# Products of the unscaled activations at six norms, with the order of ScalarE and VectorE there written out

## The chip, the cores and the metric

The kernel runs on one core of a Trainium2 chip. The metric is the device time of one execution in microseconds; the kernel before took 1698.53 us (median of three runs, 1694.67 to 1702.13). All matrix products are made in float32 accuracy from float32r operands: each operand is split in a high part `h` (rounded) and a low part `l` (the remainder), and a product is `h·h + l·h + h·l`, so three passes of TensorE (PE) for each pair of tiles.

## The reference, cut to what matters

Two blocks follow each other: the first has two layers (gated DeltaNet, then mLSTM, each with a convolved feed-forward network), the second has a SwiGLU network, a mixing stage of three branches and a second SwiGLU network. Between them stand RMS norms:

```python
def rms_norm(x, w):                                   # the same in both blocks
    y = x * rsqrt(mean(x * x, -1) + 1e-6)             # one factor for each token
    return y * w                                      # one factor for each channel
...
for i in range(2):                                    # first block, 272 tokens, 1024 channels
    mix = gated_deltanet(rms_norm(hs, norm_w[i, 0])) if i == 0 else mlstm(rms_norm(hs, norm_w[i, 0]))
    hs = hs + rms_norm(mix, norm_w[i, 1])
    f = conv_ffn(rms_norm(hs, norm_w[i, 2]))          # (silu(conv(h @ w_gate)) * conv(h @ w_up)) @ w_down
    hs = hs + rms_norm(f, norm_w[i, 3])
...
x = x + 0.5 * swiglu(rmsnorm(x, ffn1_norm), ffn1_w_gu, ffn1_w_down)   # second block, 256 tokens
z = rmsnorm(x, mix_norm) @ w_in                       # 5280 columns: gating, latents, queries, gates
x = x + merged(z) @ w_out
x = x + 0.5 * swiglu(rmsnorm(x, ffn2_norm), ffn2_w_gu, ffn2_w_down)
```

At four places an output norm, the addition to the residual and the next input norm follow each other (after DeltaNet, after the first feed-forward network, after mLSTM, after the second one); at two places (before the mixing stage and before the last SwiGLU) only an addition and an input norm stand there. These are the six norms of the title, numbered 1 to 6 below in order of time.

## The kernel before, in words

Activations lie transposed: eight tiles of 128 channels by 272 (258, 256) tokens, all in `hst`. A weight of 512 KB is loaded by SyncE into one of three `wraw` buffers; ScalarE (ACT) copies its high part to `wh`, VectorE (DVE) or GpSimd (POOL) subtracts to get the low part `wl`; `wh` and `wl` have three buffers each, so a fourth weight waits until PE has done with the first. `wload` (L355) chooses the engine of `wl`: POOL for the first loads after a norm (`POOL_FIRST`) and for every second or fourth load of some stages (`POOL_EVERY`), else DVE.

`linears_g` (L420) makes the first chunk behind a norm: four output tiles at once, 96 products over the eight tiles of its input `X`. Behind it `conv_ffn` (L1395) and `swiglu_up` (L1720) go chunk by chunk: 48 products for the gate, 48 for the up half. Output tiles lie in PSUM, in three buffers of the pool `pp` that go round, and in banks `pc0` to `pc2`, `pb0`, `pb1`. A chunk's tile is read by ACT and DVE (convolution, silu, product with the gate, split into `hh`); until then its bank is not free.

The order of PE is fixed when the kernel is built: `Threads` runs generators against a model of the engines' times and lets whichever has its operands ready go next. The other engines' order is the scheduler's, except inside `manual_schedule`, where it is the order of the code. Each engine works its own queue strictly in that order.

`mix_end` (L694) is a norm of the first four. While the last projection runs, `mix_tile` (L664) adds up squares of the output (`macc`), of the output times its norm weight (`mwacc`) and cross products with the residual (`mcross`). Ones-products on PE add them over channels (tiles `rsp`). `rstd` (L589, a logarithm and an exponential on ACT, and a Newton step on DVE where wanted) makes the factor `r` of the output norm. POOL then updates the residual (`mw` times `r`, added to `hst`), tile by tile; at the same time DVE works out the square sum of the new residual from the three sums (`sqn`, `ssq`) and the factor `r2` of the input norm with a Newton step; then DVE multiplies each tile by weight and `r2` (`xn`), ACT rounds it (high part of `xhl`) and DVE subtracts (low part). `prenorm` (L637) does the same for norms 5 and 6 without an output norm. `warm` products fill a part of the wait at norms 1 and 2; products of the memory branch (`memp`, L1808) fill a part at norms 3, 4 and 5.

`embed` (L748) starts the kernel: 32 `warm` products, the factor of the first input norm from the loaded tokens, products `xp` that transpose and scale them, and the norm weights brought into columns (`columns`, tile `vps`, copied into `pvt`).

Of the kernel before, what the change touches and what calls it, by code (L numbers as in the profile page):

```python
# [208 lines left out]
class Kern:  # L209
    def __init__(self, ctx, tc, ins, out):  # L210
# [23 lines left out]
        self.near_load = self.seg = 0  # L234
        self.gctx = ExitStack()
# [64 lines left out]
    def stt(self, out, a, s, b, op0, op1):  # L300
        self.V.scalar_tensor_tensor(out, a, s, b, op0, op1)
# [117 lines left out]

    def linears_g(self, jobs, K, X, N):  # L420

        ps = [self.ps((128, N)) for _ in range(3)] + [self.bank("pc2", (128, N), "ps")]
        for k0 in range(0, K, 4):
            hl = [self.wload(w, k0, 4, c0, 256) for w, c0, fn in jobs]
            both = list(enumerate(ps))
            for part in [both] if k0 + 4 < K else [both[:2], both[2:]]:
                for k in range(4):
                    xh, xl = X[k0 + k]
                    yield [xl]
                    for j in range(3):  # L430
                        for n, p in part:
                            w = hl[n // 2][j == 1]
                            c = slice(n % 2 * 128, n % 2 * 128 + 128)
                            self.mm(p[:], w[:, k, c], xl if j == 2 else xh, k0 + k == j == 0, k0 + k == K - 1 and j == 2)
        for n, p in enumerate(ps):
            jobs[n // 2][2](n % 2, p[:])
# [200 lines left out]
    def prenorm(self, src, wcol, N, acc):  # L637

        r = self.sm(N, "rstd", "rstd")
        yield self.part_done  # L640
        self.rstd(r[:], (yield from self.colsum_end(0, acc[1]))[:], D, NW[2])
        self.seg += 1
        self.near_load = self.nload + POOL_FIRST[self.seg]
        return self.normed(src, wcol, r, N)
# [19 lines left out]
    def mix_tile(self, m, ps, wcol, N):  # L664
# [15 lines left out]
        if m == KD - 2:  # L680
            self.th.add([self.early([self.macc, self.mwacc, self.mcross], N)])

    def prefetch(self, loads, late=None):
        for w, *a in loads:
            self.ready[w.tensor.name, a[0], a[2]] = self.wload(w, *a[:4], late=late, own=a[4] if a[4:] else None)
# [8 lines left out]
    def mix_end(self, src, wcol, N, loads=(), late=1):  # L694
# [11 lines left out]
        r = self.sm(N, "rstd", "rstd")  # L706
        r2 = self.sm(N, "rstd2", "rstd2")
        u = self.sm(N, "sqn", "y")
        X = self.xslots(N)

        def update(k, op, n=2, eng=None):
            s2 = self.hst[:, k:k + n, T - N:]
            w = self.mw[k // 2][:, k % 2:k % 2 + n, :N]
            if op == ALU.mult:
                self.tt(w, w, r[:, None, :].to_broadcast([128, n, N]), op, eng)
            else:
                self.tt(s2, s2, w, op, eng)

        low = []
# [1633 lines left out]
```

## Time and profile before

| | |
|---|---|
| median of 3 runs | 1698.53 us (1694.67 to 1702.13) |
| the profiled execution | 1692.27 us |
| its span, first to last instruction | 1690.5 us |
| PE busy | 1563.8 us (93%) |
| DVE busy | 1093.2 us (65%) |
| ACT busy | 925.3 us (55%) |
| POOL busy | 625.4 us (37%) |
| mean granted TensorE clock | 0.968 of full speed |

The share of busy time says which engine has most to do in all; it doesn't say which engine sets the pace in a given stretch. That is read from stretches around a norm: how long it takes from the last product in front of it to the 96th behind it, and what PE waits for in between.

### The profile page before, as it was taken

To read this page: it belongs to the slowest core of one execution; us is meant where nothing else is said; L and a number is where in the kernel's file an instruction comes from. 1 tells how busy PE (TensorE), PEld (TensorE's weight loads), DVE (VectorE), ACT (ScalarE), POOL (GpSimd) and SP (SyncE) were. 2 spreads that over 40 slices of the span, in tenths; PEclk is the share of its full clock that TensorE was granted. 3 is DMA by queue.
4 is the path that set the end of the run, shared out by engine and by line. 5 is a ranking of instruction groups with operands and counts; after the bars stand their busy time and mean duration, and the time that the engine had idled before them with its cause. 6 is when DMAs were issued, how large, how long until landed. Compare 5 with 4: busy or idle time off the path is not lost.

```text
span 1690.5 us, 31083 instructions
## 1 busy us (share of the span) xinstructions
PE 1563.8 (93%) x11945; PEld 1473.4 (87%) x11945; DVE 1093.2 (65%) x2121; ACT 925.3 (55%) x1877; POOL 625.4 (37%) x575
## 2 busy tenths in 40 slices
PE   8889888889899998899899998999997899999999
PEld 6778777789799997788799997999986799989987
DVE  3788977757788756357777667545459653465543
ACT  3467767656466544446566555544444664554442
POOL 2675554330500003551544444212265648512221
PEclk7889999999999999999999999999999999999999
DMA  4322221226365553444356654656554435546564
GB/s 131 101 76 63 76 64 51 76 76 198 94 182 169 170 174 93 108 120 138 109 179 188 186 176 126 199 174 194 181 161 138 115 99 151 179 147 186 181 193 150
DMA packets 239098, 235.38 MB, mean 139 GB/s; under 512 B 11510, under 2 KB 226406, under 8 KB 238950
## 3 DMA queue, kind: packets, MB, share of 16 engines
q1 hardware_dynamic: 238326, 231.86, 45.5%
q8 instruction: 94, 1.54, 0.4%
q0 software_dynamic: 496, 1.41, 0.3%
q14 instruction: 54, 0.44, 0.1%
q10 hardware_dynamic: 128, 0.13, 0.0%
HBM read 232.32 MB, written 1.05 MB: 138 GB/s over the span
## 4 chain that ended last, share of the span: by engine, by line
PE 69%; DVE 20%; ACT 5%; issue 2%; DMA 2%; POOL 1%; ACTq 0%; DVEq 0%; POOLq 0%
PE ps L190 54%; PE pst L190 5%; DVE cy L190 3%; DVE rq_a L190 3%; ACT wh L190 2%; DVE RT L190 1%; DVE wl L190 1%; DVE rq_y L190 1%; DVE xhl L190 1%; POOL wl L381 1%; DVE xn L190 1%; PE xp L190 1%; DVE nwa L190 1%; DMA wraw<-in_ffn_w_up_dram 1%; DVE on L190 1%
## 5 line engine op out<-in xcount | busy, mean ns | idle before, releaser
L190 PE MATMUL ps<-xhl,wh 128*128 128x256 f32 (+2 forms) x4624 | 882.8, 293 | 33.7 <-ACT xhl L190 17.3
L190 PEld LDWEIGHTS ps<-xhl,wh 128*128 128x128 f32 x4624 | 721.6, 192 | 43.7 <-ACT xhl L190 19.4
L190 ACT CAST wh<-wraw 128x1024 fp32r<-128x1024 f32 (+2 forms) x436 | 447.8, 1029 | 388.1 <-PE ps L190 261.4
L190 PE MATMUL ps<-xhl,wl 128*128 128x256 f32 (+2 forms) x2312 | 644.0, 287 | 1.3 <-DVE wl L190 0.8
L381 POOL TENSOR_TENSOR wl<-wraw,wh 128x512 fp32r<-128x512 f32 (+3 forms) x264 | 335.2, 1294 | 524.5 <-ACT wh L190 501.7
L190 PEld LDWEIGHTS ps<-xhl,wl 128*128 128x128 f32 x2312 | 435.6, 192 | 1.9 <-DVE wl L190 1.0
L190 DVE TENSOR_TENSOR wl<-wraw,wh 128x1024 fp32r<-128x1024 f32 (+2 forms) x237 | 289.2, 1221 | 208.4 <-ACT wh L190 202.1
L190 POOL TENSOR_TENSOR wl<-wraw,wh 128x512 fp32r<-128x512 f32 x134 | 173.9, 1320 | 145.5 <-ACT wh L190 132.8
L190 PE MATMUL ps<-hh,wh 128*128 128x256 f32 (+1 forms) x1056 | 191.1, 283 | 0.0
L190 PEld LDWEIGHTS ps<-hh,wh 128*128 128x128 f32 x1056 | 163.2, 189 | 0.0
L190 PE MATMUL ps<-hh,wl 128*128 128x256 f32 (+1 forms) x528 | 149.7, 284 | 0.0
L190 DVE SCALAR_TENSOR_TENSOR fy<-ps,pvt,fy 128x256 f32<-128x256 f32 (+2 forms) x176 | 85.0, 488 | 25.0 <-ACT fy L190 23.1
L190 PEld LDWEIGHTS ps<-hh,wl 128*128 128x128 f32 x528 | 99.5, 188 | 0.0
L190 DVE SCALAR_TENSOR_TENSOR cy<-cx,pvt,cy 128x271 f32<-128x271 f32 (+2 forms) x96 | 74.6, 780 | 14.2 <-ACT cy L190 13.2
L190 DVE TENSOR_TENSOR hh<-fy,hh 128x256 fp32r<-128x256 f32 (+1 forms) x88 | 65.2, 744 | 14.0 <-ACT hh L190 13.9
L190 POOL MEMSET mvt<- 128x4 f32 x4 | 0.4, 103 | 177.2 <-PE ps L190 177.2
L298 POOL TENSOR_TENSOR mw<-mw,rstd 128x544 f32<-128x544 f32 (+5 forms) x20 | 24.1, 1205 | 111.1 <-ACT rstd L190 111.1
L190 ACT ACTIVATE fy<-ps,pvt 128x272 f32<-128x272 f32 (+1 forms) x88 | 49.6, 569 | 12.1 <-PE ps L190 11.7
L190 PE MATMUL pst<-wh,hh 128*128 128x512 f32 x176 | 55.0, 393 | 0.0
L190 ACT CAST hh<-fy 128x256 fp32r<-128x256 f32 (+1 forms) x88 | 35.6, 406 | 29.4 <-DVE fy L190 28.8
L190 DVE CAST_PREDICATED RT<-lvl,w 128x512 f16<-128x512 uint8 x67 | 44.9, 683 | 7.1 <-PE w L190 6.9
L190 PE MATMUL ps<-og,wh 128*128 128x272 f32 x256 | 48.6, 289 | 0.1
(510 smaller groups left out, 2353.7 us busy)
## 6 DMA issues: line engine op xcount, KB each, us to landing
wraw<-in_ffn_w_up_dram SPq DMA_DIRECT2D x88, 512.0 KB
wraw<-in_ffn_w_gu_dram SPq DMA_DIRECT2D x88, 512.0 KB
wraw<-in_ffn_w_down_dram SPq DMA_DIRECT2D x79, 512.0 KB
wraw<-in_gdn_w_in_dram SPq DMA_DIRECT2D x48, 512.0 KB
wraw<-in_w_in_dram SPq DMA_DIRECT2D x41, 512.0 KB
wraw<-in_ml_w_in_dram SPq DMA_DIRECT2D x24, 512.0 KB
wraw<-in_gdn_w_out_dram SPq DMA_DIRECT2D x16, 512.0 KB
wraw<-in_ml_w_out_dram SPq DMA_DIRECT2D x8, 512.0 KB
```

What stands on the lines that cost most here:

```text
L190: r = f(*args, **kw)
L298: (eng or self.V).tensor_tensor(out, a, b, op)
L381: eng.tensor_tensor(l[:, a, b], r[:, a, b], h[:, a, b].bitcast(F32), ALU.subtract)
```

## The change

Since the factor of an input norm is the same for all channels of a token, it can be applied to the product's result. At norms 1 to 4 the residual is now updated by DVE, and ACT and DVE make the operand from the residual and the norm weight alone (`xr`, high and low part), without the factor `r2`. The factor is worked out later, on DVE behind the eight tiles (`token_scale`, called by `linears_g` through `self.mid`), and DVE multiplies each result by it when it leaves PSUM (`py`). In the two convolved networks and in mLSTM the first chunks (three, and q, k and v of the first two column blocks) use the unscaled operand, and the scaled operand `xhl` is made beside them (`scaled_operand`). In the SwiGLU networks and in the mixing stage all products use the unscaled operand, and norms 5 and 6 make it tile by tile in `add_tile`. The memory product (6, 7) moves from norm 5 into chunk 9 of the SwiGLU network in front of it. At the start there are 35 `warm` products instead of 32, and `columns` comes behind the factor of the first norm.

```diff
     def linears_g(self, jobs, K, X, N, ready=None):
         for k0 in range(0, K, 4):
-            hl = [self.wload(w, k0, 4, c0, 256) for w, c0, fn in jobs]
+            if k0 and self.mid:
+                with self.tc.issue_after(self.last_low.ins), self.tc.manual_schedule(
+                        engines={mybir.EngineType.DVE, mybir.EngineType.Activation}):
+                    hl = [self.wload(w, k0, 4, c0, 256, eng=self.V) for w, c0, fn in jobs]
+                    self.mid()
+                self.mid = None
+            else:
+                hl = [self.wload(w, k0, 4, c0, 256) for w, c0, fn in jobs]
...
     def mix_end(self, src, wcol, N, loads=(), late=1, full=True):
...
-        pb = yield from self.colsum_end(1, self.mwacc[1])
-        pa = yield from self.colsum_end(2, self.mcross[1])
+        pb = yield from self.colsum(self.mwacc, N, "pc1")
+        yield ["pc0"]
+        pa = yield from self.colsum(self.mcross, N, "pc0")
         if N == T:
-            yield from self.warm(2, self.macc[0])
+            yield from self.warm(5, self.macc[0])
...
+        def residual(n):
+            self.tt(w[n], w[n], r[:, None, :].to_broadcast([128, w[n].shape[1], N]), ALU.mult)
+            self.tt(s2[n], s2[n], w[n], ALU.add)
+        def high(*ks):
+            for k in ks:
+                self.act(raw[k][0], src[k], AF.Copy, scale=self.pv(wcol + k))
+        def low(*ks):
+            for k in ks:
+                self.last_low = self.stt(raw[k][1], src[k], self.pv(wcol + k), raw[k][0].bitcast(F32), ALU.mult, ALU.subtract)
-        with self.tc.manual_schedule(engines={mybir.EngineType.DVE, mybir.EngineType.Pool}):
+        with self.tc.manual_schedule(engines={mybir.EngineType.DVE, mybir.EngineType.Activation}):
             self.rstd(r[:], pm[:], D, NW[0])
-            for k, n in ((0, 1), (1, 1), (2, 2), (4, 2), (6, 2)):
-                for op in (ALU.mult, ALU.add):
-                    update(k, op, n, self.nc.gpsimd)
...
+            residual(0)
+            high(0)
+            residual(1)
+            high(1)
+            low(0)
+            residual(2)
+            high(2, 3)
+            low(1)
+            wlow = []
+            self.prefetch(loads[late:], wlow, self.V)
+            residual(3)
+            high(4, 5)
+            low(2, 3)
+            for f in wlow:
+                f()
+            residual(4)
+            high(6, 7)
+            low(4, 5, 6, 7)
+        def token_scale():
             self.tt(u[:], pb[:], r[:], ALU.mult)
...
-            if N == T:
-                yield from self.warm(7, c)
             self.rstd(r2[:], c, D, NW[1])
-            for k in range(0, KD, 2):
...
+        self.mid = token_scale
+        return raw, self.scaled_operand(src, wcol, N) if full else None
+    def scaled(self, p, N=S):
+        y = self.sm(N, "py")
+        self.tt(y[:], p, self.r[:], ALU.mult)
+        return y[:]
...
     def embed(self):
-            for _ in range(32):
+            for _ in range(35):
                 self.mm(p[:], self.zero[:, :128], self.zero[:])
...
-            self.columns(self.norms, 0)
             self.tt(ss[:, 0, :], ss[:, 0, :], ss[:, 1, :], ALU.add)
...
+            self.columns(self.norms, 0)
...
     def conv_ffn(self, X, l, N, lead):
-                y = conv(p, 2 * c + m)
+                y = conv(self.scaled(p, N) if c < 3 else p, 2 * c + m)
...
+                    ps = [self.bank(b, (128, N), "ps") for b in ("pc0", "pc1")] if c == 1 and fn is gate else None
+                    yield from self.linear_g(W, c0, 256, KD, x, N, fn, ps)
+                    if len(X) < KD:
+                        X = next(todo) and next(todo)
...
     def ml_gates(self, X, done):
+        yield [self.r[:], "pb1"]
+        p = self.bank("pb1", (128, 3, 128), "mrp")
+        for t, (o, P) in enumerate(TT):
+            self.tr(p[:P, t, :], self.r[:, o:o + P])
...
     def add_tile(self, m, ps, scale):
-        self.stt(x, ps, scale, x, ALU.mult, ALU.add)
+        if scale == 0.5:
+            y = self.sm(S, "ady", "y")
+            self.stt(y[:], ps, scale, self.r[:], ALU.mult, ALU.mult)
+            self.tt(x, x, y[:], ALU.add)
+        else:
+            self.stt(x, ps, scale, x, ALU.mult, ALU.add)
+        h, l = self.nextX[m]
+        self.act(h, x, AF.Copy, scale=w)
+        self.stt(l, x, w, h.bitcast(F32), ALU.mult, ALU.subtract)
...
     def mem_kv(self):
-        for n, js in enumerate(((0, 1), (2, 3), (6, 7))):
+        for n, js in enumerate(((0, 1), (2, 3))):
```

The order on VectorE at norm 1, before: from the last cross product (`cross`) straight to the square sum of the new residual (`sqn`, `ssq`), the Newton step (`nwv`, `nwa`, `rstd`) and the first scaled tiles (`xn`).

```order
L190 TENSOR_TENSOR cross<-hst,mw 128x272
L190 TENSOR_TENSOR sqn<-rsp,rstd 128x272
L190 SCALAR_TENSOR_TENSOR sqn<-rsp,sqn 128x272
L190 TENSOR_TENSOR sqn<-sqn,rstd 128x272
L190 TENSOR_TENSOR ssq<-sqn,ssq 128x272
L190 TENSOR_SCALAR nwv<-ssq 128x272
L190 TENSOR_TENSOR nwa<-rstd_5992 128x272
L190 TENSOR_TENSOR nwa<-nwa,nwv 128x272
L190 SCALAR_TENSOR_TENSOR rstd_5992<-nwa,rstd_5992 128x272
L190 SCALAR_TENSOR_TENSOR xn<-hst,pvt,rstd_5992 128x272 x2
L190 TENSOR_TENSOR xhl<-xn,xhl 128x272 x2
```

The same place after: the residual (`mw`, `hst`), which POOL had, and the low parts of the unscaled operand (`xr`).

```order
L190 TENSOR_TENSOR cross<-hst,mw 128x272
L190 TENSOR_TENSOR mw<-mw,rstd 128x272
L190 TENSOR_TENSOR hst<-hst,mw 128x272
L190 TENSOR_TENSOR mw<-mw,rstd 128x272
L190 TENSOR_TENSOR hst<-hst,mw 128x272
L190 SCALAR_TENSOR_TENSOR xr<-hst,pvt,xr 128x272
L190 TENSOR_TENSOR mw<-mw,rstd 128x544
L190 TENSOR_TENSOR hst<-hst,mw 128x544
L190 SCALAR_TENSOR_TENSOR xr<-hst,pvt,xr 128x272
```

Further on in the same stretch after: the last low parts, the low part of the last weight of the first chunk, the factor, and the first results that leave PSUM.

```order
L190 SCALAR_TENSOR_TENSOR xr<-hst,pvt,xr 128x272 x4
L190 TENSOR_TENSOR wl<-wraw,wh 128x1024
L190 TENSOR_TENSOR sqn<-rsp,rstd 128x272
L190 SCALAR_TENSOR_TENSOR sqn<-rsp,sqn 128x272
L190 TENSOR_TENSOR sqn<-sqn,rstd 128x272
L190 TENSOR_TENSOR ssq<-sqn,ssq 128x272
L190 TENSOR_SCALAR nwv<-ssq 128x272
L190 TENSOR_TENSOR nwa<-rstd_6006 128x272
L190 TENSOR_TENSOR nwa<-nwa,nwv 128x272
L190 SCALAR_TENSOR_TENSOR rstd_6006<-nwa,rstd_6006 128x272
L190 TENSOR_TENSOR py<-ps,rstd_6006 128x272 x2
```

The factor `r2` (`rstd_6006`, `rstd_5992` before) has moved from in front of the operand to behind it; nothing of a result can be read before it.

The order on ScalarE at norm 4, after (`xr` high parts; `memkt` copies of the memory branch's keys, `junk` their squares; four weights, then the factor `rstd_13078`):

```order
L190 ACTIVATE rstd<-rstd 128x256
L190 ACTIVATE xr<-hst,pvt 128x256 x4
L190 CAST wh<-wraw 128x1024
L190 COPY memkt<-memp 128x512
L190 ACTIVATE xr<-hst,pvt 128x256 x2
L190 COPY memkt<-memp 128x512
L190 ACTIVATE junk,memks<-memkt 128x128 x7
L190 ACTIVATE xr<-hst,pvt 128x256 x2
L190 ACTIVATE junk,memks<-memkt 128x128
L190 CAST wh<-wraw 128x1024 x4
L190 ACTIVATE rstd_13078<-ssq,epst 128x256
```

Seven squares of the memory branch stand in front of the last two high parts, and four weights in front of the factor's logarithm; before, that logarithm stood behind one weight.

The order on PE at norm 2 (mLSTM), before: the transposes of the gate row (`mgp`) stand among the products of the first chunk and wait for no factor.

```order
L190 MATMUL ps<-xhl,wh 128x272 x4
L190 MATMUL ps<-xhl,wl 128x272 x4
L190 MATMUL ps<-xhl,wh 128x272 x4
L190 MATMUL mgp<-eye,gr 128x8 x2
L190 MATMUL mgp<-eye,gr 16x8
L190 MATMUL ps<-xhl,wh 128x272 x4
```

The same place after: transposes of the factor (`mrp`) in front of the last products of the first chunk and of `mgp`.

```order
L190 MATMUL ps<-xr,wl 128x272 x2
L190 MATMUL ps<-xr,wh 128x272 x2
L190 MATMUL mrp<-eye,rstd_8621 128x128 x2
L190 MATMUL mrp<-eye,rstd_8621 16x128
L190 MATMUL ps<-xr,wh 128x272 x2
L190 MATMUL ps<-xr,wl 128x272 x2
L190 MATMUL ps<-xr,wh 128x272 x4
L190 MATMUL ps<-xr,wl 128x272 x2
L190 MATMUL ps<-xr,wh 128x272 x2
L190 MATMUL mgp<-eye,gr 128x8 x2
L190 MATMUL mgp<-eye,gr 16x8
```

PE's queue now waits for `r2` here, with 12 products of the first chunk behind it.

## Rows read from the trace of the kernel before

**Rows 1.** The page: busy time by engine; chain of waits, shares by engine.
```profile
PE 1563.8 (93%) x11945; PEld 1473.4 (87%) x11945; DVE 1093.2 (65%) x2121; ACT 925.3 (55%) x1877; POOL 625.4 (37%) x575
...
PE 69%; DVE 20%; ACT 5%; issue 2%; DMA 2%; POOL 1%; ACTq 0%; DVEq 0%; POOLq 0%
```
**Rows 2.** Stretches: window, length, busy of PE, PEld, DVE, ACT, POOL; clock, DMA, GB/s.
```profile
428.90:458.60 29.70, 22.44 (x126) 19.83 (x126) 21.72 (x30) 11.93 (x22) 18.14 (x15) 0.89 0.18 54
648.00:688.50 40.50, 27.34 (x169) 23.12 (x168) 29.47 (x58) 13.37 (x27) 19.29 (x16) 0.85 0.23 66
808.50:838.10 29.60, 22.36 (x133) 19.62 (x132) 22.24 (x37) 11.78 (x23) 16.74 (x15) 0.88 0.22 70
1021.30:1049.70 28.40, 22.16 (x132) 19.75 (x132) 22.04 (x41) 15.36 (x40) 14.85 (x13) 0.88 0.30 94
1234.40:1255.60 21.20, 20.54 (x144) 18.12 (x143) 11.85 (x26) 10.83 (x22) 13.43 (x15) 1.00 0.48 140
1492.00:1512.00 20.00, 16.75 (x118) 15.70 (x119) 11.75 (x25) 12.10 (x23) 1.97 (x2) 0.91 0.29 87
478.00:490.00 12.00, 12.00 (x98) 12.00 (x97) 10.05 (x17) 7.63 (x12) 0.00 (x0) 1.00 0.60 175
440.90:447.80 6.90, 5.61 (x23) 5.29 (x24) 6.83 (x10) 1.67 (x4) 3.04 (x3) 0.51 0.01 2
```
**Rows 3.** In order of time at norm 1: start, length, engine, operation [idle before <-releaser].
```profile
428.58 0.29 PE L190 MATMUL ps<-og,wl 128*128 128x272 f32 x1
...
429.72 0.43 ACT L190 ACTIVATE sq<-mw 128x272 f32<-128x272 f32 x1
...
431.26 0.43 ACT L190 ACTIVATE rstd<-rstd 128x272 f32<-128x272 f32 x1
...
431.72 0.44 DVE L190 TENSOR_TENSOR sqn<-rsp,rstd 128x272 f32<-128x272 f32 x1 [1.56 <-ACT rstd L190]
...
436.89 1.46 DVE L190 TENSOR_TENSOR nwa<-nwa,nwv 128x272 f32<-128x272 f32 x1
438.01 1.52 POOL L298 TENSOR_TENSOR mw<-mw,rstd 128x544 f32<-128x544 f32 x1
...
441.82 1.27 PE L190 MATMUL ps<-xhl,wh 128*128 128x272 f32 x4 [3.65 <-ACT xhl L190]
...
450.96 2.00 ACT L190 CAST wh<-wraw 128x1024 fp32r<-128x1024 f32 x2 [2.13 <-PE ps L190]
```
**Rows 4.** Groups by shape on DVE: count, busy, mean ns (first three from 478:490).
```profile
L190 DVE TENSOR_TENSOR wl<-wraw,wh 128x1024 fp32r<-128x1024 f32 x4 | 4.9, 1225 | 1.8 <-ACT wh L190 1.6
L190 DVE SCALAR_TENSOR_TENSOR fy<-ps,pvt,fy 128x270 f32<-128x270 f32 x4 | 2.0, 497 | 0.1
...
L190 DVE TENSOR_TENSOR hh<-fy,hh 128x272 fp32r<-128x272 f32 x3 | 1.3, 435 | 0.0
...
L190 DVE TENSOR_TENSOR meml<-wraw,memh 128x512 fp32r<-128x512 f32 x16 | 10.9, 686 | 4.2 <-ACT memh L190 3.9
```
**Rows 5.** In order of time behind norm 1, POOL, DVE and PE.
```profile
461.81 2.75 POOL L381 TENSOR_TENSOR wl<-wraw,wh 128x512 fp32r<-128x512 f32 x2 [1.47 <-ACT wh L190]
...
462.06 2.79 DVE L190 TENSOR_TENSOR fy<-fy,sg 128x272 f32<-128x272 f32 x2
...
467.78 0.49 PE L190 MATMUL ps<-xhl,wh 128*128 128x272 f32 x2 [1.46 <-DVE fy L190]
```
**Rows 6.** Who waited for whom: engine, for what, us, times, longest.
```profile
PE mbp L190 <- DVE mlf L190: 5.3, 1, 5.3
```
**Rows 7.** In order of time at norm 4, ACT.
```profile
1030.16 0.31 ACT L190 ACTIVATE junk<-memkt 128x128 f32<-128x128 f32 x1
1030.37 0.19 ACT L190 ACTIVATION_READ_ACCUMULATOR junk<-memkt 128x1 f32 x1
```
**Rows 8.** Start, in order of time (ACT, PE, DVE), and one stretch as in rows 2.
```profile
8.19 0.19 ACT L190 ACTIVATION_READ_ACCUMULATOR junk<-xt 128x1 f32 x1
...
11.72 0.23 DVE L190 COPY pvt<-vps 128x64 f32<-128x64 f32 x1 [3.79 <-PE vps L190]
...
14.65 13.57 PE L190 MATMUL xp<-rd,xt 128*128 128x128 f32 x48 [2.97 <-DVE rd L190]
...
14.30:34.80 20.50, 19.67 (x75) 16.07 (x76) 7.36 (x15) 3.90 (x8) 2.20 (x4) 0.50 0.42 119
```

More of the change, by code (lines that the diff above doesn't have):

```diff
@@ L312, in act @@
             self.order(inst)
+        return inst
     def split(self, h, l, src):
@@ L635, in normed, with token_scale @@
         return X
-    def prenorm(self, src, wcol, N, acc):
-        r = self.sm(N, "rstd", "rstd")
+    def token_scale(self, acc, N, done):
         yield self.part_done
[L641 to L644, printed above, removed]
+        p = yield from self.colsum_end(0, acc[1])
+        r = self.r = self.sm(N, "rstd", "rstd")
+        self.rstd(r[:], p[:], D, NW[2])
+        yield [r[:], "pc0"]
+        p = self.bank("pc0", (128, 2, 128), "rtp")
+        for t in range(2):
+            self.tr(p[:, t, :], r[:, t * 128:t * 128 + 128])
+        rt = self.rt = self.cst([128, 2], name="rtok", tag="al")
+        self.V.tensor_copy(rt[:], p[:, :, 0])
+        done.set()
     def sumsq(self, go, then):
@@ L680, in mix_tile, with prefetch @@
         if m == KD - 2:
[L681 to L683 removed]
+            self.th.add([self.early([self.macc], N)])
+    def prefetch(self, loads, late=None, eng=None):
         for w, *a in loads:
[L685 removed]
+            self.ready[w.tensor.name, a[0], a[2]] = self.wload(w, *a[:4], late=late, own=a[4] if a[4:] else None, eng=eng)
     def warm(self, n, x):
@@ L1625, in mlstm @@
         self.lane = None
-        yield from self.linears_g([job("q", 0), job("k", 0)], KD, X, T)
+        yield from self.linears_g([job("q", 0), job("k", 0)], KD, raw, T)
+        X = next(todo) and next(todo)
         for kind, n in (("v", 0), ("v", 1), ("q", 1), ("k", 1), ("v", 2), ("v", 3), ("o", 0), ("o", 1), ("o", 2), ("o", 3)):
@@ L1631, in mlstm @@
             else:
-                yield from self.linear_g(w, c0, 256, KD, X, T, fn)
+                yield from self.linear_g(w, c0, 256, KD, raw if (kind, n) in raws else X, T, fn)
+                while len(X) < KD:
+                    next(todo)
+                    if len(X) in (5, 8):
+                        break
         return Y
@@ L1718, in all, with swiglu_up @@
                 return e.value
-    def swiglu_up(self, X, w, extra=None):
+    def swiglu_up(self, X, w, extra=None, late=False, ready=None):
         Y = []
@@ L1737, in swiglu_up @@
             if c == 0:
-                yield from self.linears_g([(w, 0, gate), (w, FF, up)], KD, X, S)
+                yield from self.linears_g([(w, 0, gate), (w, FF, up)], KD, X, S, ready)
             else:
-                yield from self.linear_g(w, c * 256, 256, KD, X, S, gate)
+                ps = [self.bank(b, (128, S), "ps") for b in ("pc0", "pc1")] if c == 1 else None
+                yield from self.linear_g(w, c * 256, 256, KD, X, S, gate, ps)
                 yield from self.linear_g(w, FF + c * 256, 256, KD, X, S, up)
```

127 lines of the change are left out of this document (73 added, 54 removed).

## The prediction

> **What bounds the kernel now.** I read the page first, then one table of stretches, then the order of time around a norm. On the page PE is busy 93% of the span and holds 69% of the chain of waits, DVE 20% [rows 1]: away from the norms PE sets the pace. The steady chunk shows it: 98 products in 12.00 us without a hole, 0.1224 us each, so 96 cost 11.75 us [rows 2]. There DVE is busy 10.05 of 12 us, which matters below.
>
> The table of stretches then runs, for each of the six norms, from the last product in front of it to the 96th behind it. Norm 1 takes 29.70 us for 11.75 us of products, norms 3 and 4 29.60 and 28.40, norm 6 20.00. Norm 2 takes 40.50 us; its stretch holds 24 gate products and a wait for the gates besides. Norm 5 takes 21.20 us, but PE is busy for 20.54 of them: products of the memory branch fill it [rows 2].
>
> The order of time at norm 1 tells why. The last product ends at 428.87 us, the factor's exponential at 431.69, and the first product behind the norm begins only at 441.82: 10.1 us in which DVE works out the second factor beside POOL's residual. There a DVE step that takes 0.44 us alone takes 1.46 [rows 3]. PE then starts at half its clock: 0.51 in the 6.9 us from 440.9 [rows 2], the 1.2 GHz level.
>
> **The change, part by part.**
>
> *First chunk at norms 1 to 4.* ACT's last square ends at 430.15 [rows 3]; logarithm and exponential (some 1.0 us) end at 431.2. Then DVE has, in the order shown: four residual steps of 272 columns, 0.5 us each with the hand-over (2.0); six of 544, from 686 ns for 512 [rows 4] 0.75 each (4.5); eight low parts, 0.45 each from 435 to 497 ns (3.6); one weight remainder, 1.22. Sum 11.3 us, so the last low part ends at 442.5. Two weights of 1.0 us each (2.00 for two [rows 3]) stand before the last two high parts on ACT and wait for PE to leave the first half; I add 1.0: 443.5. The remainder of the last weight, 1.22, ends at 444.7, and 22 to 24 products still come: 447.5. POOL meanwhile takes the next weights; if each of DVE's last steps meets it, 3 us more, 450.5. The 96th product then stands 18.6 to 21.6 us behind the last one in front, against 29.70: 8 to 11 us gained there. The two to five extra warm products and the longer sums fill idle PE: nothing.
>
> *What gives part of it back.* Each result must now wait for `r2`. Behind 444.7 stand eight steps on DVE and two on ACT, 4.5 us alone, up to 10 beside POOL: `r2` at 449 to 455. In chunks 0 to 2 DVE gets twelve multiplications and eight scaled tiles besides. From `r2` to the step that frees the bank of chunk 3's second tile stand 59 DVE instructions: 6 remainders at 1.225 and 53 others at 0.40 (in the steady chunk 13 take 10.05 − 4.9 us [rows 2, 4]), 28.6 us, so 477.8 to 483.6. Before, chunk 3 began at 458.6 + 2 × 11.75 + the 1.46 us of [rows 5] = 483.6, its second tile 1.5 later. So norm 1 keeps 1.5 to 7.3 us; I take 5, the nearer to DVE without POOL, since four loads alone go to POOL. Norm 3 has the same order: 5, range 1 to 8.
>
> A row shows what POOL does to such steps: two of 272 columns took 2.79 us beside a POOL remainder of 2.75 [rows 5], where one alone takes 0.435 [rows 4]. The Trainium skill ("SBUF — State Buffer", section "SBUF: two separate sides") says that a VectorE instruction with two SBUF inputs and a GpSimd instruction exclude each other for their whole length; the trace agrees (1.46 against 1.52 us in turn, rows 3). It speaks against part of this change: the residual leaves POOL, but POOL's four weights now fall on the steps that make `r2`. By it alone `r2` comes at 455 and norm 1 keeps 1.5 us.
>
> *Norm 2.* PE's queue waits for `r2` with 12 products of the chunk behind it, then gates behind that. `r2` at 449 to 455 in norm 1's times, with the same steps; the gate chain from there took PE's 5.3 us wait [rows 6] and lasts as long as before. So the wait for the gates ends about when it did, but 138 products of the projections stand before it where 84 stood: 54 × 0.1224 = 6.6 us are out of the way. I take 5 (0 to 8): what follows is partly a chain of its own.
>
> *Norm 4.* The first chunk as at norm 1, but seven squares of 0.5 us (0.31 + 0.19 [rows 7]) stand before ACT's last high parts: 3.5 us, gain there 7 instead of 9. Then the logarithm of `r2` waits behind four weights, the last of which needs a buffer that PE leaves after the first chunk, and four remainders of the memory branch (0.69 each [rows 4]) stand among the Newton steps. PE has 48 products (5.9 us) in banks of its own, then waits; I put 4 us on it. Gain 3 (−2 to 8). Behind it DVE is light: its multiplications hide under PE.
>
> *Norms 5 and 6.* Seven of eight tiles are ready before the last product, the eighth needs four short steps, some 2.2 us, covered by 84 products. Norm 5 had 0.7 us idle, and its memory products now stand elsewhere at the same cost: 1 (−1 to 2). Norm 6: 20.00 us for 11.75 × 256/272 = 11.1 us of products, 2.5 of transposes and 0.9 of sums: 5.5, and with a clock of 0.91 there [rows 2] I take 6 (4 to 7). The multiplications in SwiGLU and the mixing stage, 68 of about 0.42 us, lie on a DVE with 65% load: nothing, up to 3 if a chain passes through them.
>
> *Start.* The factor's data are ready at 8.38, but DVE stood behind `pvt`, which waited 3.79 us for PE's warm products [rows 8]. The factor comes 3.3 us earlier; warm products (three more, 0.7 us) end at 12.2, and `xp` begins at 12.4 instead of 14.65: 2.2 us. PE had 0.50 of its clock for the 20.50 us from 14.30, though busy for 19.67 [rows 8]; the level fell after the hole of 2.97 us that now closes. If it stays up for the first quarter of `xp`, 1.7 us more: 4 in all; if throughout, half of 13.57 and of the rest, 11. The skill ("TensorE: Matmul & The Clock Gate", Part 1) lets the clock follow how busy PE is; by that it would stay up, while the row shows 96% busy at half the clock. I side with the row.
>
> **Sum.** 4 + 5 + 5 + 5 + 3 + 1 + 6 = 29 us. The profiled execution took 1692.27 us (its span 1690.5), so 1663 in its terms; the runs' median, 1698.53, lies 0.37% above it, and in its terms 1669.5. I say 1669. The bounds of single terms add up to +4 and +51; they will not all fall to one side.
>
> **The rivals.**
>
> *DVE becomes the bound (slower).* Place: chunks 0 to 2 behind norms 1 and 3, the wait for `r2` at norms 2 and 4. DVE there already has 84% load; with 14 us more in three chunks it has over 100%. Price: if the list of 28.6 us runs 1.5 times as long (POOL, waits for ACT), chunk 3 starts some 12 us later than forecast, and a PE hole like the 3.65 us one sets the clock to half for 6.9 us, 3.4 us more. Three such places cost 46 against 29 saved: 1698.5 + 17 = 1715. It decides once the list passes 37 us. For it: the 1.46 us waits behind DVE in [rows 5]. Against it: POOL has four loads, not all.
>
> *The gain stays half.* Norms 1 and 3 keep 1.5 by the exclusion of POOL and DVE, norm 2 keeps 2, norm 4 nothing, the start 2.2, norm 6 5.5: 13 us, 1685.
>
> *Everything fits.* DVE's list hides under PE, no hole lowers the clock: norms 1 to 4 keep 8 each, the start 7, norms 5 and 6 8: 47 us, 1651. Against it: DVE's 46 us of steps from norm 1 to chunk 3 in a stretch of 50.
>
> *It doesn't do what it says.* A first product that still waits for `r2` would give nothing, 1698. The order shows `xr` ahead of the factor, so this is unlikely.
>
> **How the numbers follow.** Forecast (1658 to 1680): 0.48. Half (1680 to 1690): 0.20. Everything fits: 0.14. Nothing left or nothing done (1690 to 1707): 0.11. Slower: 0.07. About 0.5% (8.5 us) is what a measurement can tell here; below 1690 is 0.82, within 0.11, above 1707 0.07. The range leaves out less than 2 in 10: from the middle of the fourth case to the third's, 1650 to 1692.
>
> **What would show it.** Right: the first product behind norm 1 follows the last one in front by about 5 us instead of 13, and the 96th by 19 to 22. `r2` ends 20 to 26 us behind the last product. PE waits for DVE (`py`) in chunks 1 to 3, some us per norm; for `rstd` at norm 2. At norm 6 no hole in front of the first product. `xp` begins near 12.4. Wrong: holes over 10 us in front of chunks 1 to 3, a clock below 0.9 there, or a first product that still waits for `xhl`.

## The result, and the profile after

The changed kernel took 1682.47 us (median of 5 runs, 1679.54 to 1685.82), the kernel before 1696.51 us in runs beside it (median of 5, 1694.67 to 1702.13). The ratio is 0.991, 95% interval 0.989 to 0.994: about 14 us faster, where 29 were forecast. The time lies inside the range given (1650 to 1692), but in the interval of the rival "the gain stays half" (1680 to 1690, given 0.20) and not in that of the forecast (1658 to 1680, given 0.48); the place of the gain is not where either of them had it.

The page after, busy time by engine, answers to [rows 1]:

```profile
PE 1557.9 (93%) x11939; PEld 1470.2 (87%) x11939; DVE 1141.3 (68%) x2284; ACT 936.2 (56%) x1893; POOL 576.6 (34%) x531
```

Stretches after (window, length, busy of PE, PEld, DVE, ACT, POOL; clock, DMA, GB/s), to be held against [rows 2, 8]: the start; norm 1 from the last product in front to the 96th behind it, and from there to the start of chunk 3; the same two at norm 3; norm 4.

```profile
14.30:34.80 20.50, 19.00 (x128) 16.71 (x129) 11.29 (x22) 8.65 (x17) 7.99 (x9) 0.92 0.42 118
415.80:436.10 20.30, 18.23 (x119) 16.13 (x118) 16.41 (x25) 9.76 (x17) 4.95 (x4) 1.00 0.25 76
436.10:470.20 34.10, 25.95 (x195) 25.70 (x194) 32.09 (x63) 22.29 (x38) 6.18 (x5) 0.90 0.45 141
790.60:811.00 20.40, 19.93 (x134) 18.29 (x133) 17.23 (x33) 10.42 (x20) 3.85 (x3) 1.00 0.34 103
811.00:845.20 34.20, 25.28 (x193) 24.86 (x193) 32.65 (x60) 21.26 (x37) 10.47 (x9) 0.85 0.39 123
1012.00:1031.20 19.20, 19.20 (x132) 17.80 (x132) 15.45 (x31) 12.89 (x35) 3.98 (x4) 1.00 0.38 114
```

Two readings. The first 96 products behind norms 1, 3 and 4 now take about 20.3, 20.4 and 19.2 us, against 29.7, 29.6 and 28.4: the part of the change that was meant works. The 192 products behind them take 34 us where 23.5 us of work stand, and DVE is busy for 94 and 95% of that time.

Counting products from the last one in front of a norm gives the same in one table (start of the n-th product, us; a few records can be missing, so tenths are rough):

| | 96th | 192nd | 240th | 288th (chunk 3) | 384th |
|---|---|---|---|---|---|
| norm 1 before | 29.6 | 43.4 | 49.4 | 55.4 | 67.4 |
| norm 1 after | 20.2 | 32.3 | 48.2 | 54.2 | 66.3 |
| norm 3 before | 29.5 | 43.0 | 48.8 | 54.6 | 66.1 |
| norm 3 after | 20.2 | 31.8 | 48.4 | 54.5 | 72.1 |
| norm 4 before | 28.3 | 39.7 | 46.9 | 52.6 | 64.0 |
| norm 4 after | 19.2 | 39.1 | 45.7 | 51.4 | 62.8 |

A lead of 9 to 11 us is there, and is given back between the 192nd and the 240th product (at norm 4 between the 96th and the 192nd). The rows of PE at those places, in order of time (start, length, engine, operation [idle before <-releaser]): norm 1's first product, then the waits at norms 1, 2, 3 and 4 and in the mixing stage.

```profile
420.78 0.87 PE L190 MATMUL ps<-xr,wh 128*128 128x272 f32 x4
...
458.08 0.82 PE L190 MATMUL ps<-xr,wh 128*128 128x272 f32 x2 [8.15 <-DVE py L190]
...
656.85 0.90 PE L190 MATMUL mrp<-eye,rstd 128*128 128x128 f32 x3 [4.93 <-DVE rstd L190]
...
832.89 0.80 PE L190 MATMUL ps<-xr,wh 128*128 128x258 f32 x2 [8.85 <-DVE py L190]
...
1042.94 0.77 PE L190 MATMUL ps<-xr,wh 128*128 128x256 f32 x2 [5.76 <-DVE py L190]
...
1282.64 0.58 PE L190 MATMUL ps<-xhl,wh 128*128 128x256 f32 x1 [6.42 <-DVE py L190]
```

What stands in front of the 8.15 us on DVE, in order of time at norm 1 (groups between the rows left out): the factor's sums beside POOL's remainders, the last steps of `r2`, the convolution beside POOL again, and the multiplication that frees the bank; below them POOL's remainders in that time.

```profile
433.61 0.44 DVE L190 SCALAR_TENSOR_TENSOR sqn<-rsp,sqn 128x272 f32<-128x272 f32 x1
434.09 1.36 DVE L190 TENSOR_TENSOR sqn<-sqn,rstd 128x272 f32<-128x272 f32 x1
435.48 1.41 DVE L190 TENSOR_TENSOR ssq<-sqn,ssq 128x272 f32<-128x272 f32 x1
...
438.42 0.44 DVE L190 TENSOR_TENSOR nwa<-nwa,nwv 128x272 f32<-128x272 f32 x1
438.89 0.44 DVE L190 SCALAR_TENSOR_TENSOR rstd<-nwa,rstd 128x272 f32<-128x272 f32 x1
...
440.56 2.92 DVE L190 SCALAR_TENSOR_TENSOR fy<-py,pvt,fy 128x271 f32<-128x271 f32 x2 [0.34 <-ACT fy L190]
...
457.60 0.43 DVE L190 TENSOR_TENSOR py<-ps,rstd 128x272 f32<-128x272 f32 x1
```

```profile
433.87 2.72 POOL L383 TENSOR_TENSOR wl<-wraw,wh 128x512 fp32r<-128x512 f32 x2 [2.08 <-ACT wh L190]
438.93 5.70 POOL L383 TENSOR_TENSOR wl<-wraw,wh 128x512 fp32r<-128x512 f32 x4 [2.34 <-DVE nwa L190]
```

`r2` ends at 439.33, 23.5 us behind the last product (20 to 26 forecast). From there DVE works until 458.03 with about 1 us of pauses in all, and 0.05 us later PE goes on. PE had finished 204 products of the norm, which is two chunks and the first half of chunk 2's first tile; the second tile needs the first bank of the round pool again, and that holds an up half of chunk 1 which DVE reads only here.

At the start, the rows that answer to [rows 8]: `xp` follows the last warm products at once and takes 7.76 us instead of 13.57.

```profile
12.24 7.76 PE L190 MATMUL xp<-rd,xt 128*128 128x128 f32 x48
```

Where the time came from and went, from the two profiled executions (1692.27 and 1685.52 us, so only 6.75 us apart; the one of after lies at the upper end of its runs). Lead of after over before at the last product in front of norm 1: 13.1 us; norm 2: 14.3; norm 3: 18.0; norm 4: 9.3; at the 96th product behind norm 5: 10.2; in front of norm 6: 2.4; at the end 6.75. So start and DeltaNet +13.1, norm 1 +1.2, norm 2 +3.7, norm 3 −8.7, norms 4 and 5 +0.9, mixing stage −7.8, norm 6 +4.4.

One pair of traces gives this only roughly: traces of the same code differ by up to 7 us in a section (the mixing stage of before took 235.7 to 242.5 us). In the means of all traces that share a section's code (three with that of before; four with that of after, six for the mixing stage) norm 1 stands at +0.6, norm 2 at +4.7, norm 3 at −7.1, norms 4 and 5 at +2.8, the mixing stage at −4.8, norm 6 at +3.4: together about nothing.

### The profile page after: what moved, and what is told of

It is laid out like the page before. It is cut to its first block, busy times and chain, and to the rows that moved or that the text cites. A ratio compares the mean times of both kernels' runs of the same rounds, so it can differ in the third digit from the quotient of the medians.

```text
span 1683.7 us, 31234 instructions
## 1 busy us (share of the span) xinstructions
PE 1557.9 (93%) x11939; PEld 1470.2 (87%) x11939; DVE 1141.3 (68%) x2284; ACT 936.2 (56%) x1893; POOL 576.6 (34%) x531
## 4 chain that ended last, share of the span: by engine, by line
PE 39%; DVE 9%; DMA 3%; ACT 3%; issue 1%; POOL 1%; ACTq 0%; POOLq 0%; DVEq 0%
PE ps L190 31%; PE pst L190 5%; ACT wh L190 1%; DVE wl L190 1%; PE memp L190 1%; DVE fy L190 1%; DVE rq_a L190 1%; DMA wraw<-in_ffn_w_up_dram 1%; DMA wraw<-in_ml_w_out_dram 1%; DVE rq_y L190 1%; DMA wraw<-in_mem_w_kv_dram 1%; POOL wl L383 1%; DVE qtok L190 1%; DVE qsq L190 1%; PE rsp L190 0%
## 5 line engine op out<-in xcount | busy, mean ns | idle before, releaser
L190 PE MATMUL ps<-xhl,wh 128*128 128x272 f32 (+2 forms) x3280 | 639.8, 295 | 19.7 <-DVE py L190 8.3
L190 PEld LDWEIGHTS ps<-xhl,wh 128*128 128x128 f32 x3280 | 514.5, 192 | 25.9 <-DVE py L190 8.7
L190 PE MATMUL ps<-xhl,wl 128*128 128x272 f32 (+2 forms) x1640 | 465.1, 288 | 0.8 <-POOL wl L383 0.8
L190 DVE TENSOR_TENSOR wl<-wraw,wh 128x1024 fp32r<-128x1024 f32 (+3 forms) x239 | 289.1, 1210 | 180.8 <-ACT wh L190 176.2
L190 PEld LDWEIGHTS ps<-xhl,wl 128*128 128x128 f32 x1640 | 312.2, 192 | 1.2 <-POOL wl L383 1.2
L190 PE MATMUL ps<-xr,wh 128*128 128x256 f32 (+2 forms) x1216 | 225.3, 293 | 25.0 <-DVE py L190 23.0
L190 PEld LDWEIGHTS ps<-xr,wh 128*128 128x128 f32 x1216 | 191.8, 197 | 27.7 <-DVE py L190 18.2
L190 PE MATMUL ps<-xr,wl 128*128 128x256 f32 (+2 forms) x608 | 164.1, 291 | 1.1 <-DVE wl L190 1.1
L190 PEld LDWEIGHTS ps<-xr,wl 128*128 128x128 f32 x608 | 114.0, 196 | 1.6 <-DVE wl L190 1.5
L190 DVE TENSOR_TENSOR hh<-fy,hh 128x256 fp32r<-128x256 f32 (+1 forms) x88 | 63.8, 728 | 11.7 <-ACT hh L190 11.6
L190 DVE TENSOR_TENSOR py<-ps,rstd 128x256 f32<-128x256 f32 (+2 forms) x96 | 39.9, 423 | 37.8 <-PE ps L190 37.5
```

What stands on the lines that cost most here:

```text
L190: r = f(*args, **kw)
```

## The experiments

Each stands beside runs of the kernel before on the same chip; its median was 1696.06 to 1698.68 us in the four sets.

**The start alone, and all but the start.** To before: 35 warm products and `columns` behind the factor. To after: the reverse.

```diff
-            for _ in range(32):
+            for _ in range(35):
...
-            self.columns(self.norms, 0)
...
                 self.ts(rd[:P, t, :P], self.ident[:P, :P], r[:P, t:t + 1], ALU.mult)
+            self.columns(self.norms, 0)
```

> The kernel before with the start of the changed one alone (35 warm products, norm vectors copied behind the factor). Theory A (the start holds the clock up, and the DeltaNet stage behind it keeps the lead and adds some; it brought 13 us of the change): 13 us less than before, 1683 to 1686, xp begins at 12.2 us at full clock, the half-clock stretch of 20.5 us shrinks to under 7 us, and the feed-forward stretch behind norm 1 begins about 13 us earlier. Theory B (the term of the prediction, 4 us, and the rest of the lead belongs to other parts of the change): 1692 to 1693.

> The changed kernel with the start of before (32 warm products, norm vectors copied in front of the factor). Theory A: nearly the whole gain goes, 1693 to 1697, since the six norms and the mixing stage together bring about 1 us. Theory B (the start is worth 4, the norms some 10): 1686 to 1687.

Measured: the start alone 1686.12 us (ratio 0.993, 0.991 to 0.995), all but the start 1696.51 us (1.000, 0.999 to 1.002). Theory A holds: three warm products and one moved copy bring 11 of the 14 us; which of the two does it, no run separates. All the rest of the change brings nothing that can be told from zero where it stands alone, and the 3 to 4 us that it adds on top of the start aren't clear of the noise either (ratios 0.991, 0.989 to 0.994, and 0.993, 0.991 to 0.995). The start's stretch with the edit alone:

```profile
14.30:34.80 20.50, 19.00 (x131) 16.70 (x130) 11.61 (x22) 8.48 (x17) 8.42 (x10) 0.92 0.45 129
```

**The clock or the earlier beginning?** To before, behind the transposes of the norm vectors:

```diff
             self.columns(self.norms, 0)
+            for _ in range(13):
+                self.mm(p[:], self.zero[:, :128], self.zero[:])
```

> The kernel before, with 13 more warm products on PE behind the transposes of the norm vectors, where it waited 2.97 us in front of xp; nothing comes earlier by it. Theory A (the hole drops the clock for the 20.5 us that follow, and the earlier beginning is worth only 2.4 us of the start): xp begins at about 14.7 us as before but at full clock, and the kernel is 6 to 9 us faster than before, 1688 to 1691. Rival B (xp's products run at half clock whatever stands in front, and the changed start won by beginning earlier): 1696 to 1699.

Measured: 1691.42 us (ratio 0.998, 0.996 to 0.999). In its trace `xp` begins when it did before, but at 2.4 GHz; first its row, then the stretch of [rows 8].

```profile
14.74 1.45 PE L190 MATMUL xp<-rd,xt 128*128 128x128 f32 x8 [1.80 <-DVE rd L190]
```

```profile
14.30:34.80 20.50, 18.74 (x122) 16.32 (x123) 9.37 (x21) 7.47 (x15) 6.07 (x8) 0.92 0.44 121
```

The lead at the end of `xp` is 5.7 us in the trace, all of it the clock; in the runs 4 us remain by the ratio (1 to 7 by its interval) and 5.6 by the medians, a little under the 6 to 9 expected. Rival B falls: `xp` isn't bound to half the clock. Of the start's 8.2 us at that point in the changed kernel, 2.4 are the earlier beginning and 5.8 the clock. The kernel with all but the start shows the low level a second time, here behind a hole of 4.95 us:

```profile
15.79 13.42 PE L190 MATMUL xp<-rd,xt 128*128 128x128 f32 x48 [4.95 <-DVE rd L190]
```

```profile
14.30:34.80 20.50, 18.53 (x77) 15.35 (x78) 8.26 (x22) 3.90 (x8) 2.08 (x4) 0.58 0.43 120
```

**The factor taken out of the convolved networks** (results of chunks 0 to 2 left unscaled):

```diff
-                y = conv(self.scaled(p, N) if c < 3 else p, 2 * c + m)
+                y = conv(p, 2 * c + m)
```

(and the same in `up`)

> The changed kernel without the multiplication by the factor in the first three chunks of both convolved networks (the factor is left out of these results; the scaled operand is still made). Theory A (norms 1 and 3 give their lead back because chunk 2's second tile waits for a bank that VectorE frees only behind r2 and its list): the waits of 8.15 and 8.85 us in front of that tile go, each norm keeps 6 to 11 us, 1660 to 1670. Rival C (VectorE has too much to do in chunks 0 to 2 in any order, or the scaled operand comes too late for chunk 3): the waits move to chunk 3 and shrink by no more than the 24 multiplications of 0.43 us, 1675 to 1681.

Measured: 1673.92 us, 8.6 under the changed kernel, between the two expectations. The waits shrink but stay, now for the convolution itself:

```profile
452.39 0.79 PE L190 MATMUL ps<-xr,wh 128*128 128x272 f32 x2 [4.62 <-DVE fy L190]
```

The 240th product behind norm 1 starts at 44.7 us instead of 48.2, so of the 9 to 11 us given back the wait for `r2` and the multiplications account for 3.5 at norm 1; what is left waits for DVE's convolution, as the row says. (Without the multiplication a bank is free only behind the convolution's last read, so the two kernels differ in that too.) At norm 3 the 384th product comes at 63.8 us instead of 72.1.

**Other banks, and the factor early.** First: chunk 2's tiles to banks that are free by then. Second: sums, logarithm and exponential of `r2` into the place where DVE idles in front of the last two low parts.

```diff
+                    if c == 2 and fn is gate:
+                        ps = [self.ps((128, N)), self.bank("pc2", (128, N), "ps")]
```

(and `pc0`, `pc1` for the up half of chunk 2)

```diff
-            low(4, 5, 6, 7)
+            low(4, 5)
+            self.tt(u[:], pb[:], r[:], ALU.mult)
...
+            newton = self.rstd_begin(r2[:], c, D)
+            low(6, 7)
```

(`newton`, the last three steps, stands where the whole factor stood)

> The changed kernel, with the third chunk behind norms 1 and 3 written to other banks: its gate half to one of the round pool and pc2 (free since 446.4 us), its up half to pc0 and pc1. Theory A (the wait of 8.15 and 8.85 us is for the one bank that comes round, whose reader stands late on VectorE): the waits fall under 3 us, each of the two norms keeps 5 more, 1671 to 1674. Rival C (VectorE's list itself is the bound, the scaled operand for chunk 3 is ready only at 473 us): the wait moves to chunk 3, 1680 to 1684.

> The changed kernel, with the sums, the logarithm and the exponential of the factor r2 written ahead of the last two low parts (VectorE waits 1.82 us there at norm 1), and only the last three Newton steps behind the last weight. Theory A (norms 1 to 4 give back what r2 comes late): r2 comes 3 to 5 us earlier, the waits of 8.15, 4.93, 8.85 and 5.76 us shrink by 3 to 4 each, 1668 to 1673. Rival C (VectorE's list behind r2 is the bound at norms 1 and 3, so only what it waited or ran slowly beside GpSimd is won): 2 us each at norms 1 and 3, 3 each at norms 2 and 4, 1672 to 1675. Rival D (the factor isn't what is waited for): 1681 to 1684.

Measured: banks 1681.61 us (ratio 0.991, 0.989 to 0.992), no change against after. Its 288th product behind norm 1 starts at 44.9 us instead of 54.2, so the wait did go; the 384th at 68.0 instead of 66.3. PE with the other banks, in chunk 3:

```profile
464.56 0.39 PE L190 MATMUL ps<-xhl,wh 128*128 128x272 f32 x1 [0.57 <-ACT xhl L190]
466.71 0.40 PE L190 MATMUL ps<-xhl,wh 128*128 128x272 f32 x1 [1.76 <-DVE xhl L190]
...
469.31 0.59 PE L190 MATMUL ps<-xhl,wh 128*128 128x272 f32 x1 [1.14 <-DVE xhl L190]
...
471.87 0.59 PE L190 MATMUL ps<-xhl,wh 128*128 128x272 f32 x1 [1.75 <-ACT xhl L190]
```

Rival C: the wait moved to the scaled operand that chunk 3 reads. The early factor gave 1676.92 us (0.987, 0.985 to 0.989). Its `r2` at norm 1 ends 19.2 us behind the last product in front (23.5 in after); the wait there is 4.62 us, at norm 4 it is gone (192nd product at 30.7 us instead of 39.1), at norm 2 it is 2.95 instead of 4.93. The time lies above both theory A and rival C, 2 us over C: the factor's lateness is a part of the loss, 5.6 us of it, and not the whole.

**The mixing stage.** The factor left out of the gating branch's first projection; or, with the factor, the low parts of its four weights on DVE instead of POOL:

```diff
-            yield from self.linear_g(W, n * 256, 256, KD, X, S, lambda m, p: self.act(u[:, m, :], self.scaled(p), AF.Gelu))
+            yield from self.linear_g(W, n * 256, 256, KD, X, S, lambda m, p: self.act(u[:, m, :], p, AF.Gelu))
```

```diff
+        if eng is None and self.force:
+            eng = self.V
...
+            self.force = True
             yield from self.linear_g(W, n * 256, 256, KD, X, S, lambda m, p: self.act(u[:, m, :], self.scaled(p), AF.Gelu))
+            self.force = None
```

> The changed kernel without the multiplication by the factor in the first projection of the mixing stage's gating branch (512 columns, factor left out; ScalarE reads the bank itself, as before). Theory A (the mixing stage lost 8 us because this multiplication stands on VectorE behind some 20 us of small Newton steps): the wait of 6.42 us at 1276 us goes and the stage keeps its lead, 1674 to 1678. Rival C (the Newton steps are late themselves, so PE waits for the queries instead, as the kernel before did for 6.72 us): 1680 to 1683.

> The changed kernel, with the low parts of the four weights of the gating branch's projection in the mixing stage on VectorE instead of GpSimd. Theory A (there GpSimd slows VectorE's small steps from 0.15 to 1.2 us, some 13 of them, so that the multiplication stands 6 us late): the list gets 13 us shorter and 4.9 longer, the wait of 6.42 us goes, 1674 to 1678. Rival C (the steps are slow by their own dependence, and VectorE only gets more to do): 1683 to 1688.

Measured: 1680.53 and 1682.60 us (0.990, 0.988 to 0.992, and 0.991, 0.989 to 0.992): neither can be told from the changed kernel. In both the wait of 6.42 us is gone and another has taken its place; in turn, the row without the factor and the row with DVE's low parts:

```profile
1291.46 0.88 PE L190 MATMUL qktp<-eye,qtok 128*96 128x128 f32 x3 [9.41 <-DVE qtok L190]
```

```profile
1290.56 0.66 PE L190 MATMUL qktp<-eye,qtok 128*96 128x128 f32 x2 [7.85 <-DVE qtok L190]
```

Without the factor it is rival C: the queries themselves are late. With DVE's low parts the time lies just under rival C, but not for its reason: with fewer of POOL's remainders beside them the 18 steps on one number per partition took 0.33 us each in the mean instead of 0.66, so they weren't slow by their own dependence; here too the queries are what PE then waits for.

**All three edits** (banks, early factor, DVE's low parts in the mixing stage):

> The three edits together (other banks, the factor early, the mixing stage's four low parts on VectorE). If each acts in its own place and as theory A has it, the gains add up: 1656 to 1664. If the two edits at norms 1 and 3 win the same time, 1662 to 1668. If VectorE is the bound everywhere, 1676 to 1684.

Measured: 1672.45 us (0.985, 0.983 to 0.987), 4.5 under the early factor alone, which the two intervals don't separate. None of the three forms fits; chunk 3 still waits for the scaled operand (384th product at 65.3 us behind norm 1, 68.7 behind norm 3). The row behind norm 1:

```profile
470.33 0.59 PE L190 MATMUL ps<-xhl,wh 128*128 128x272 f32 x1 [4.08 <-ACT xhl L190]
```

**Less on DVE.** On top of these three: the low parts that POOL makes just behind norms 1 and 3 to DVE (the first diff). Or: no scaled operand at norms 1 and 3 at all (the second).

```diff
-POOL_FIRST = (0, 4, 2, 2, 0, 0, 0)
+POOL_FIRST = (0, 0, 2, 0, 0, 0, 0)
...
+            self.near_dve = self.nload + 10 if self.seg == 3 else 0
```

```diff
-                y = conv(self.scaled(p, N) if c < 3 else p, 2 * c + m)
+                y = conv(self.scaled(p, N), 2 * c + m)
...
-            x = raw if c < 3 else X
+            x = raw
```

> The kernel with all three edits (1672.5), with the low parts of the weights loaded just behind norms 1 and 3 on VectorE instead of GpSimd (four weights at norm 1, some six at norm 3). Theory A (a GpSimd remainder beside VectorE costs it as much as or more than the 1.22 us that it takes over: at norm 3 some 12 us of slowed steps for 7.3 us): no change at norm 1, chunk 4 behind norm 3 begins 3 to 5 us earlier, 1666 to 1670. Rival C (GpSimd's help is net): VectorE's list gets 5 and 7 us longer, 1678 to 1684.

> The kernel with all three edits (1672.5), with no scaled operand at norms 1 and 3: all 11 chunks take the unscaled one, and every result is multiplied (16 VectorE and 8 ScalarE steps fewer in chunks 0 to 2, four multiplications of 0.43 us more in each of the eight later chunks). Theory A (VectorE's list in chunks 0 to 2 is the bound, 7.2 us of it the scaled operand): the waits of 4 us behind norm 1 and 7 behind norm 3 in front of chunk 3 go, 1661 to 1667. Rival C (the later chunks then bring VectorE to 11.8 of 12 us and its backlog never drains): holes in every later chunk, 1674 to 1690.

Measured: DVE instead of POOL 1670.95 us (0.986, 0.984 to 0.988), no difference from 1672.45: what POOL takes over and what it slows are about equal. Without the scaled operand 1661.12 us (0.980, 0.978 to 0.981), the best of all, 21 us under the changed kernel and 36 under before. Behind norm 1 PE then runs without a hole at full clock from chunk 1 on:

```profile
437.20:461.30 24.10, 24.10 (x195) 24.10 (x194) 21.62 (x40) 17.06 (x26) 5.85 (x4) 1.00 0.57 171
```

The 384th product starts 58.3 us behind norm 1 (66.3 in after), 60.6 behind norm 3 (72.1). This edit does three things at once: DVE has 16 steps fewer, ACT 8, and chunk 3 no longer reads an operand that is made late. The run doesn't separate them.

**No scaled operand, alone on the changed kernel** (the second diff again):

> The changed kernel with one edit: no scaled operand at norms 1 and 3, all 11 chunks take the unscaled one. Theory A (VectorE's list behind the factor is the bound, and the 16 steps of the scaled operand, of which some 9 stand before the late bank comes free, are its surplus): the waits of 8.15 and 8.85 us fall to some 4 each, those in front of chunk 3 behind norm 3 go, 1669 to 1674. Rival C (bank and late factor are what holds PE, the scaled operand only fills VectorE's gaps): 1679 to 1684. Rival D (the multiplications of the later chunks cost what the scaled operand saved): 1682 to 1690.

Measured: 1675.26 us (0.988, 0.986 to 0.991), 7 under the changed kernel; the profiled execution has the waits at 4.97 and 4.78 us and the 384th product behind norm 3 at 62.2 us. That is 1 us above what theory A gave and 4 below rival C; rivals C and D fall. The edit is worth 7 us alone and 11 on top of the other three, which are worth 10 without it and 14 with it. The waits at norms 1 and 3:

```profile
452.38 0.82 PE L190 MATMUL ps<-xr,wh 128*128 128x272 f32 x2 [4.97 <-DVE py L190]
...
823.82 0.71 PE L190 MATMUL ps<-xr,wh 128*128 128x258 f32 x2 [4.78 <-DVE py L190]
```

These two stand in chunk 2, which never read the scaled operand, so the 3.2 and 4.1 us by which they fell, the edit's 7 us, come from a shorter list in front of the bank. On top of the three edits what goes is a wait for the scaled operand itself.

## Why the prediction was right in sign and wrong in its terms

*First chunk at norms 1 to 4: right.* First product 5.0 us behind the last one in front at norm 1 (5 forecast), the 96th at 20.2 (18.6 to 21.6); at norm 4 9.1 us gained there (7 forecast).

*What gives part of it back: the step that failed.* The prediction counted DVE's list from `r2` to chunk 3 (28.6 us) and let PE meet it there, with chunk 2 done. PE meets it a chunk earlier, at chunk 2's second tile, so 84 products (10.3 us) stand behind the wait and not in front of it, the first of them at half clock (6.8 us at half from 454.5, 3.3 of them behind the hole). Norm 1 kept 1.2 us (5 forecast, 1.5 to 7.3). Norm 3 was put down as the same; there the lead was gone at chunk 3, and 6 us more by the 384th product. That is the mechanism of the rival "DVE becomes the bound", at the place it names: at norm 3 for about its price (−8.7 where 5 were forecast), at norm 1 for less. Another bank only moves the wait. The early factor brought 5.6 us, the multiplications left out 8.6, the scaled operand left out 7 alone and 11 on top of the three edits: each takes something out of DVE's list or puts it into a pause, and none alone lets the whole lead stay. That fits a bound by the sum of DVE's work in chunks 0 to 2, not by the one row that PE waits for; for the 11 us the late operand may be a cause beside it.

*POOL beside DVE.* The rows agree with the Trainium skill ("SBUF — State Buffer", section "SBUF: two separate sides"): `nwa<-nwa,nwv` took 1.46 us beside POOL before [rows 3] and 0.44 after, between two of POOL's remainders, while `sqn<-sqn,rstd` beside one of them took 1.36. The 1.5 us that the forecast put down by it alone is close to the 1.2 measured, but that doesn't make it the cause: with those remainders on DVE the time stayed the same (1670.95 against 1672.45). That run shows that POOL's help and its price are about equal, not what the exclusion costs by itself.

*Norm 2* kept 3.7 us (5 forecast, 0 to 8), with the wait for `rstd` at `mrp` as foretold. *Norm 4 and norm 5* together 0.9 (4 forecast; 2.8 in the means above): the wait came after the 48 products behind the first chunk, as foretold, but was 5.76 us instead of 4 and took the clock with it, 6.8 us at half. The memory branch's remainders stand among the Newton steps, as the prediction had it; what it missed is that the copy in front of them (`memh` on ACT) waited for its load. ACT, then DVE, in order of time:

```profile
1038.98 1.14 ACT L190 CAST memh<-wraw 128x512 fp32r<-128x512 f32 x2 [3.60 <-DMA wraw<-in_mem_w_kv_dram]
```

```profile
1037.51 0.42 DVE L190 TENSOR_TENSOR nwa<-nwa,nwv 128x256 f32<-128x256 f32 x1
1039.63 1.29 DVE L190 TENSOR_TENSOR meml<-wraw,memh 128x512 fp32r<-128x512 f32 x2 [1.70 <-ACT memh L190]
1040.84 0.42 DVE L190 SCALAR_TENSOR_TENSOR rstd<-nwa,rstd 128x256 f32<-128x256 f32 x1
```

The last Newton step waits 2.9 us for nothing that it needs. With the factor early the whole wait is gone. *Norm 6* kept 4.4 (6 forecast, 4 to 7; 3.4 in the means above), without a hole in front of its first product; behind the first two PE waits 1.00 us for DVE's `hst`.

*Elsewhere, costed at nothing: wrong.* From norm 5's 96th product to the last one in front of norm 6 the unchanged mixing stage took 235.7, 240.0 and 242.5 us in three traces (before, and the two of before with another start), the changed one 243.2 to 246.6 in six; 241.7 without that multiplication and 239.8 to 243.1 in four with DVE's low parts. So the stage lost about 5 us in the mean, and about half of it goes with either edit, though the runs' times show neither. The rest shows as queries that come 3 us later; why is not settled.

*Start: the sign of the choice was wrong.* 4 us were put down, 2 to 11 allowed; 8.2 stood at the end of `xp`, 13 in front of norm 1, 11 in the runs. I sided with the row that showed half the clock at 96% busy, against the Trainium skill ("TensorE: Matmul & The Clock Gate", Part 1), by which the clock follows how busy PE is. The row showed what came after a hole, not what `xp` does: with the hole closed, or only shortened from 2.97 to 1.80 us by idle products, the same `xp` runs at 2.4 GHz. By the page's rule the term would have been 11, and the runs agree with that, in part by luck: up to 35 us the start gave 8.8. Why the level then stayed low for 20.5 us with PE busy for 96% of them, no run shows; by the page's rule alone it should have risen. Of the rest of the lead 3 us come between 260 and 367 us, 2.1 of them where a hole of 4.04 us (first row, before) became one of 1.97 (second row, after):

```profile
356.65 0.82 PE L190 MATMUL ps<-xhl,wh 128*128 128x272 f32 x2 [4.04 <-DVE zs L190]
...
344.36 0.52 PE L190 MATMUL ps<-xhl,wh 128*128 128x272 f32 x2 [1.97 <-DVE zs L190]
```

The same hole is 1.96 us with the start alone and 4.04 with more warm products; why, no run shows.

That the time lies inside the range is luck: two errors partly cancel. In the runs the start was counted 7 us too low (4 for 11) and all else 22 or more too high (25 for 3 on top of the start, for nothing alone). The range's own sum is a little off as well: the low bounds of the terms add up to about 5.5 us, not 4, or 2.5 with the 3 us allowed for chains elsewhere.

## What to carry to other kernels

When work moves off the critical path onto an engine that is 84% busy, add up what that engine has to do from the moment it is late until it can be level again, and ask which consumer meets it first; a wait's named releaser is only the first of several in that queue, and freeing it moves the wait. Prefer to take work away (here: the second form of one operand, 7 and 11 us) over reordering it (other banks nothing, an earlier factor 5.6). And look for holes of a few microseconds in front of long runs of products early in a kernel: three dummy products and a copied vector moved behind a factor were worth more here than all the rest of the change.

## What the runs showed of the hardware

A hole of 2.97 us in front of `xp` was followed by 20.5 us at 1.2 GHz though PE was busy for 19.67 of them [rows 8]; with 1.80 us idle in front of it the same products ran at 2.4 GHz, and a hole of 1.32 us behind them was followed by 3.4 us at half. In the mixing stage DVE steps of one number per partition, 0.15 us alone, took mostly about 1.2 us beside POOL's remainders; a row of each from the changed kernel:

```profile
1264.38 1.17 DVE L190 TENSOR_TENSOR rq_a<-rq_a,rq_v 128x1 f32<-128x1 f32 x1
...
1277.62 0.15 DVE L190 TENSOR_TENSOR rq_a<-rq_a,rq_v 128x1 f32<-128x1 f32 x1
```

```profile
1264.24 12.83 POOL L383 TENSOR_TENSOR wl<-wraw,wh 128x512 fp32r<-128x512 f32 x10 [2.18 <-ACT wh L190]
```

The first of the two DVE rows lies inside POOL's stretch (1264.24 to 1277.07), the second just behind it.
